# A hybrid SSD and attention layer: norm sums from token layout, paired SSD output weights, four-head v tiles and a third weight pair

## The chip, the core and the metric

The kernel is one launch on one core of a Trainium2 chip. The core has five engines with instruction streams of their own: TensorE (PE) for matmuls, VectorE (DVE), ScalarE (ACT), GpSimd (POOL) and SyncE (SP), which here issues most DMAs. They work on SBUF (128 partitions) and on PSUM, where matmuls put their sums. The metric is the time of one execution on the device in microseconds, as the median over runs; lower is better. The traces come from single profiled executions.

## What is computed

One decoder layer on 512 tokens of width 1024, in float32. The input is normalised and projected; the columns of the projection feed a Mamba-2 SSD mixer (16 heads, four chunks of 128 tokens) and a forgetting attention (16 heads of 64). Both results go through one output projection and are added to x; then come a second norm and a gated MLP with a causal convolution of width 3.

```python
h = rms_norm(x, norm_mix_w)
proj = h @ w_in
z, xbc, dt_raw, q, k, v, f_raw = jnp.split(
    proj, [Z_END, XBC_END, DT_END, Q_END, K_END, V_END], axis=-1)
y_ssd = ssd_mixer(xbc, z, dt_raw, ...)   # conv width 4, SiLU, chunked scan, gated group norm
y_fox = fox_mixer(q, k, v, f_raw, ...)   # q and k normed per head, decay added to the logits, softmax
mixed = jnp.concatenate([y_ssd, y_fox], axis=-1)
x = x + mixed @ w_out
hf = rms_norm(x, norm_ffn_w)
x = x + conv_gated_mlp(hf, w_up, ffn_conv_w, ffn_conv_b, w_down)
```

## The kernel before

**Precision.** Each large product is done in float32r, in three passes (`mm3`, lines 108 to 113): a value is split into a high part and the rest, and high x high, high x low and low x high are summed in PSUM. So every weight tile (128 x 1024) is loaded by SP into one of five `wraw` buffers, copied to its high part `wh` by ScalarE (line 104), and subtracted to its low part `wl` (line 105) by VectorE or POOL. `load_split` does this. Which engine subtracts is written out by hand in `LOW_PART` (line 36): each key is a kind of load, and the letters are taken in turn, `d` for VectorE and `p` for POOL; a key that is missing means POOL, and a call may name the engine itself. `wh` and `wl` have two buffers each.

**PSUM.** Eight banks of 128 x 512: three in the pool `g` (`bank()`: feature tiles, token blocks with two banks each, output projection), four in `m` (`mbank()`: scan, attention, transposes), one called `o`.

**The start.** x comes in transposed (`xT`, features on partitions), in eight blocks. Each is scaled by the norm's weight and split to `xh` and `xl` (line 180). The norm's factor per token comes later, since it is only a factor on the projection's results: it needs the sum of squares of each token. The squares of the eight blocks are taken by ScalarE (blocks 1, 3, 5, 7) and POOL (the others) at lines 203 to 208, added on VectorE (line 235), and summed over the partitions by four small matmuls with a column of ones into the bank `spin` (line 238). `token_scale` (line 137) turns the sums into `r`, the factor with tokens on partitions, and `R`, the same with tokens along the free axis: VectorE, a power on POOL, a diagonal on VectorE (line 140), a matmul with ones (line 144, `rbc`), a ScalarE copy (line 145).

**SSD.** `feature_tile` makes 128 columns of xbc for all tokens, in 24 matmuls. `early` (line 603) names tiles that are started ahead of `dt_f`, the chain for dt and the forget gates: tile 8 (made with the eight x blocks), 10 and 0. `ssd_proj` (line 336) makes the other tiles of a group of eight heads, multiplies each by R, runs the convolution and SiLU on VectorE and ScalarE and transposes; then it makes the gate z by token blocks. `ssd_scan` (line 386) runs over four chunks and leaves `m`, four feature blocks of 128 in high and low parts.

**Output projection.** `out_proj(pairs, m, halves)` (line 243) takes weight tiles of two feature blocks ("pair") by 512 columns ("half"). For each token block it sums over the pairs given to it in one bank and adds the bank to `x2`, which holds x in token layout (line 255). It was called with one pair at a time: pairs 0 and 1 for SSD group 0 while group 1 is scanned, pairs 2 and 3 for group 1, 4 to 7 for the attention groups.

**Attention.** `token_block` (line 319) makes q, k or v of four heads for all tokens in two banks, with 96 matmuls of 256 columns. `v_proj` (line 472) scales v by `r` and splits it, on ScalarE and VectorE in turn, for two heads at a time. Heads run in order; `fillers` (line 645) lists which projections are emitted ahead of which head.

**MLP.** 44 feature tiles up, gating, then a down projection of seven products; the weights' sums are built by accumulating DMAs of POOL's queue (line 730) whose descriptors use a scratch of 2048 bytes (line 973). `split_unit` (line 734) takes weight pairs from the two of `wp`, and each third from a pair in the pool `pb`.

**Order.** Each engine runs its instructions in a fixed order. It is made by the framework when the program is built: it simulates the kernel and takes what is ready, by priority; work under `high_priority` goes first, else what was emitted first. So an edit in one place can change the order elsewhere.

Of the kernel before, what the change touches and what calls it, by code (L numbers as in the profile page):

```python
# [8 lines left out]
F32 = mybir.dt.float32  # L9
# [46 lines left out]
def tile_hybrid_layer(  # L56
# [105 lines left out]
    first = [wp.tile([P, 1024], F32R, tag=t, name=t) for t in ("wh", "wl")]  # L162
# [34 lines left out]
    sqs = []  # L197
    for k in range(NK):
        xr = load_x(k)
        if k == 0:  # L200
            nc.sync.dma_start(pc[:, 0:NK], pcol[:, 0:NK])
        split_x(k, xr)
        sq = px.tile([P, SEQ], F32, tag="sq", name="sq", bufs=NK)
        if k in ACT_SQ:
            act.activation(sq, xr, AF.Square)
        else:
            pool.tensor_tensor(out=sq, in0=xr, in1=xr, op=ALU.mult)
        sqs.append(sq)
        if k in (1, 3):
            split_first(*load_first(k // 2))  # L210
# [22 lines left out]
    second = load_split(wxbc[10], sub=low_part("second"))  # L233
    for k in range(1, NK):
        dve.tensor_add(sqs[0], sqs[0], sqs[k])
    with tc.high_priority(AHEAD):
        for tb in range(NTB):
            pe.matmul(spin[:, tb : tb + 1], sqs[0][:, tb * P : (tb + 1) * P], ones[:, 0:1], start=True, stop=True)
        token_scale(r, R, spin[:, 0:NTB], px)
# [3 lines left out]
    def out_proj(pairs, m, halves=(0, 1)):  # L243
        for half in halves:
            ws = [load_split(wout[pair, half], sub=low_part("o%d" % pairs[0])) for pair in pairs]
            for tb in range(NTB):
                s = slice(tb * P, (tb + 1) * P)
                o = bank("po")
                for n, (h, l) in enumerate(ws):
                    for j in range(2):  # L250
                        k = 2 * n + j
                        c = slice(j * 512, (j + 1) * 512)
                        mm3(o, m[k][0][:, s], m[k][1][:, s], h[:, c], l[:, c], k == 0, k == 2 * len(pairs) - 1)
                dst = x2[:, tb, half * 512 : (half + 1) * 512]
                dve.tensor_add(dst, o, dst)  # L255
# [729 lines left out]
```

## Time and profile before

| what | value |
|---|---|
| median of 3 runs | 828.99 us (828.06 to 830.2) |
| the profiled execution | 829.39 us, its span 827.6 us |
| mean granted TensorE clock | 0.999 |
| DMA | 98.23 MB, mean 119 GB/s |
| weight splits, ScalarE part (line 104) | 103 of 1052 ns |

The span runs from the first to the last instruction. A group of instructions is shown as line, engine, operation, output<-inputs with partitions x elements, count, then busy time and mean duration in ns, then the idle time of the engine just before them and what ended it. PEld is TensorE's weight load, which overlaps its matmuls. A wait is shown as the engine and line that waited, what for, then us in total, times, longest. Matmuls are pipelined and their ends are modelled, so a busy TensorE is not one at its peak.

### The profile page before, as it was taken

The numbers are of one execution on the slowest core, as the hardware profiler recorded it, in microseconds if no ns is written. First come the engines' busy times: TensorE is split into PE (matmuls) and PEld (weight loads), VectorE is DVE, ScalarE is ACT, GpSimd is POOL, SyncE is SP. The second block draws the span as 40 slices with busy tenths as digits, with TensorE's granted clock in tenths as the row PEclk, the third lists the DMA queues.
The fourth block names the chain that finished last, engine by engine and source line by source line (L and its number), as shares of the span: only waits on it lengthen the run. The fifth ranks groups of instructions, "written<-read, shape, count | busy, mean of one in ns | idle before, by whom it ended". The sixth has DMA issues, their size and how long they took to land.

```text
span 827.6 us, 12438 instructions
## 1 busy us (share of the span) xinstructions
PE 807.4 (98%) x4599; PEld 698.7 (84%) x4599; DVE 629.7 (76%) x1017; ACT 437.2 (53%) x847; POOL 293.8 (36%) x281
## 2 busy tenths in 40 slices
PE   8999989899999999999999999999999999999997
PEld 5788879779999998798898888888888888888886
DVE  7597898676789788997988767667666666887844
ACT  5346655534478675684575364344443344556532
POOL 4125343364565445126132514322333333143120
PEclk9999999999999999999999999999999999999999
DMA  8424323241333332333322263332233223499983
GB/s 308 164 92 132 102 77 104 89 144 60 102 116 104 114 103 79 110 94 126 103 81 74 77 165 116 101 102 81 98 102 102 100 84 96 116 248 194 208 185 94
DMA packets 31405, 98.23 MB, mean 119 GB/s; under 512 B 4016, under 2 KB 5104, under 8 KB 31344
## 3 DMA queue, kind: packets, MB, share of 16 engines
q1 hardware_dynamic: 27456, 85.38, 31.8%
q0 software_dynamic: 3456, 11.54, 7.8%
q8 instruction: 36, 0.59, 0.3%
q10 hardware_dynamic: 432, 0.52, 0.2%
q14 instruction: 25, 0.20, 0.1%
HBM read 91.56 MB, written 2.20 MB: 113 GB/s over the span
## 4 chain that ended last, share of the span: by engine, by line
PE 80%; DVE 10%; issue 3%; ACT 3%; DMA 2%; POOL 1%; SPq 0%; DVEq 0%; POOLq 0%; ACTq 0%
PE up L111 29%; PE pq L111 16%; PE po L111 10%; PE Y L111 5%; PE Z L111 4%; PE X L111 4%; DVE xs L352 2%; PE g L111 2%; PE o L586 2%; PE pT L572 2%; DMA sc<-cs_d 1%; PE yd L416 1%; PE S L546 1%; PE S L545 1%; DVE wl L105 1%
## 5 line engine op out<-in xcount | busy, mean ns | idle before, releaser
L104 ACT CAST wh<-wraw 128x1024 fp32r<-128x1024 f32 x103 | 108.3, 1052 | 137.7 <-PE up L111 72.1
L111 PE MATMUL pq<-wh,xl 128*128 128x256 f32 x512 | 146.3, 286 | 0.0
L111 PE MATMUL pq<-wh,xh 128*128 128x256 f32 x512 | 146.0, 287 | 0.0
L111 PE MATMUL pq<-wl,xh 128*128 128x256 f32 x512 | 145.1, 284 | 0.0
L111 PE MATMUL up<-hh,wl 128*128 128x512 f32 (+1 forms) x368 | 140.2, 381 | 0.2 <-DVE wl L105 0.2
L111 PE MATMUL up<-hl,wh 128*128 128x512 f32 (+1 forms) x368 | 139.9, 380 | 0.0
L111 PE MATMUL up<-hh,wh 128*128 128x512 f32 (+1 forms) x368 | 139.8, 380 | 0.0
L105 POOL TENSOR_TENSOR wl<-wraw,wh 128x1024 fp32r<-128x1024 f32 x31 | 76.7, 2474 | 107.4 <-ACT wh L104 98.4
L105 DVE TENSOR_TENSOR wl<-wraw,wh 128x1024 fp32r<-128x1024 f32 x72 | 90.7, 1259 | 20.5 <-ACT wh L104 20.4
L111 PEld LDWEIGHTS pq<-wl,xh 128*128 128x128 f32 x512 | 97.6, 191 | 1.3 <-issue 0.5
L111 PEld LDWEIGHTS pq<-wh,xh 128*128 128x128 f32 x512 | 97.2, 191 | 1.8 <-issue 1.2
L111 PEld LDWEIGHTS pq<-wh,xl 128*128 128x128 f32 x512 | 97.6, 191 | 0.7 <-issue 0.5
L111 PEld LDWEIGHTS up<-hh,wl 128*128 128x128 f32 x368 | 69.2, 188 | 13.8 <-DVE wl L105 0.4
L111 PEld LDWEIGHTS up<-hh,wh 128*128 128x128 f32 x368 | 69.1, 188 | 13.2 <-issue 0.2
L111 PEld LDWEIGHTS up<-hl,wh 128*128 128x128 f32 x368 | 69.2, 188 | 13.0
L779 DVE TENSOR_TENSOR up<-up,R 128x512 f32<-128x512 f32 x44 | 30.3, 691 | 57.0 <-PE up L111 57.0
L784 DVE SCALAR_TENSOR_TENSOR ua<-up,pc,ua 128x511 f32<-128x511 f32 (+1 forms) x88 | 67.1, 765 | 3.2 <-ACT ua L782 1.7
L532 POOL TENSOR_SCALAR bias<-cum,tokS 128x256 f32<-128x256 f32 (+1 forms) x32 | 22.6, 715 | 84.4 <-DVE nm L547 84.4
L255 DVE TENSOR_TENSOR x<-po,x 128x512 f32<-128x512 f32 x64 | 43.2, 683 | 10.1 <-PE po L111 9.5
L740 ACT CAST wh<-T 128x1024 fp32r<-128x1024 f32 (+1 forms) x30 | 29.3, 977 | 37.5 <-PE Z L111 15.6
L741 DVE TENSOR_TENSOR wl<-T,wh 128x1024 fp32r<-128x1024 f32 (+1 forms) x30 | 33.7, 1132 | 19.7 <-ACT wh L740 19.7
L794 POOL TENSOR_TENSOR ua<-ua 128x512 f32<-128x512 f32 x11 | 15.0, 1365 | 93.7 <-DVE ua L784 93.7
(239 smaller groups left out, 1885.2 us busy)
## 6 DMA issues: line engine op xcount, KB each, us to landing
wraw<-in_wup_dram SPq DMA_DIRECT2D x44, 512.0 KB, 3.3
wraw<-in_wqkv_dram SPq DMA_DIRECT2D x24, 512.0 KB, 3.4
T<-in_wdown_dram POOLq DMA_DIRECT2D x20, 512.0 KB, 7.4
wraw<-in_wout_dram SPq DMA_DIRECT2D x16, 512.0 KB, 3.4
wraw<-in_wxbc_dram SPq DMA_DIRECT2D x11, 512.0 KB, 4.0
T<-in_wdown_dram SPq DMA_DIRECT2D x10, 512.0 KB, 5.0
wraw<-in_wdown_dram SPq DMA_DIRECT2D x10, 512.0 KB, 3.6
wraw<-in_wz_dram SPq DMA_DIRECT2D x8, 512.0 KB, 3.6
```

Of the source, the lines that this page charges most:

```text
L104: act.copy(h, r)
L105: (sub or dve).tensor_tensor(out=l, in0=r, in1=raw(h), op=ALU.subtract)
L111: ins = pe.matmul(o, a, b, start=start and n == 0, stop=stop and n == 2, **kw)
L255: dve.tensor_add(dst, o, dst)
L352: dve.scalar_tensor_tensor(out=dst[:, s:], in0=xp[:, : SEQ - s], scalar=half_w[:, cw + 3 - s : cw + 4 - s], in1=dst[:, s:], op0=ALU.mult, ...
L532: (dve if qb == 2 else pool).tensor_scalar(out=b, in0=cum[:, :n], scalar1=-1.0, scalar2=edge, op0=ALU.mult, op1=ALU.add)
L572: pe.transpose(t[:, w : w + P], prob[:, o : o + P], ident)
L586: pe.matmul(cols[:m], v[:, kb, lh, vc], pt[:, s], start=kb == 0 and n == 0, stop=kb == NTB - 1, skip_group_check=True,)
L740: act.copy(h[:, :n], src[:, :n])
L741: dve.tensor_tensor(out=l[:, :n], in0=src[:, :n], in1=raw(h[:, :n]), op=ALU.subtract)
L779: dve.tensor_mul(xp, o, R2)
L784: dve.scalar_tensor_tensor(out=a[:, s:], in0=xp[:, : SEQ - s], scalar=pc[:, cw + 2 - s : cw + 3 - s], in1=a[:, s:], op0=ALU.mult, op1=ALU.add,
```

## The change

The sums of squares come from x in token layout: x2 is loaded ahead of the feature tiles, and ScalarE squares each token block with a running sum (`accum_out`), in place of eight squares, seven additions and four small matmuls. A third weight pair is split early (weights 10 and 0, now both on VectorE), and feature tile 1 joins the tiles started ahead of `dt_f`, in a bank of the pool `m`. The output projection takes the two pairs of an SSD group together: two token blocks at a time, over both weight tiles, with one addition each. v is one tile for four heads. `wh` and `wl` have three buffers everywhere, and the pair in `pb` is gone. `LOW_PART` is adapted, the fillers `a` and `b` become the two column halves `a0` and `a1` of pairs 2 and 3, and the scratch of POOL's DMA queue is halved.

```diff
-ACT_SQ = (1, 3, 5, 7)
 LOW_PART = {
     "feat": "pddddddddp",
-    "o0": "dp",
-    "o2": "dp",
+    "o0": "d",
+    "o2": "d",
     "o4": "pd",
     "o5": "pd",
+    "o6": "pd",
     "o7": "pd",
...
-        h = wp.tile([P, 1024], F32R, tag="wh", name="wh")
-        l = wp.tile([P, 1024], F32R, tag="wl", name="wl")
+        h = wp.tile([P, 1024], F32R, tag="wh", name="wh", bufs=3)
+        l = wp.tile([P, 1024], F32R, tag="wl", name="wl", bufs=3)
...
-        sq = px.tile([P, SEQ], F32, tag="sq", name="sq", bufs=NK)
-        if k in ACT_SQ:
-            act.activation(sq, xr, AF.Square)
-        else:
-            pool.tensor_tensor(out=sq, in0=xr, in1=xr, op=ALU.mult)
-        sqs.append(sq)
...
-    second = load_split(wxbc[10], sub=low_part("second"))
-    for k in range(1, NK):
-        dve.tensor_add(sqs[0], sqs[0], sqs[k])
+    second, third = [load_split(wxbc[j], sub=dve) for j in (10, 0)]
+    for tb in range(NTB):
+        nc.sync.dma_start(x2[:, tb, :], x[tb * P : (tb + 1) * P, :])
     with tc.high_priority(AHEAD):
+        ssx = px.tile([P, NTB], F32, tag="ssx", name="ssx")
         for tb in range(NTB):
-            pe.matmul(spin[:, tb : tb + 1], sqs[0][:, tb * P : (tb + 1) * P], ones[:, 0:1], start=True, stop=True)
-        token_scale(r, R, spin[:, 0:NTB], px)
+            sq = px.tile([P, D], F32, tag="sq", name="sq", bufs=2)
+            act.activation(sq, x2[:, tb, :], AF.Square, accum_out=ssx[:, tb : tb + 1])
+        token_scale(r, R, ssx, px)
...
-            for tb in range(NTB):
-                s = slice(tb * P, (tb + 1) * P)
-                o = bank("po")
+            banks = {}
+            for t0 in (0, 2):
                 for n, (h, l) in enumerate(ws):
-                    for j in range(2):
-                        k = 2 * n + j
-                        c = slice(j * 512, (j + 1) * 512)
-                        mm3(o, m[k][0][:, s], m[k][1][:, s], h[:, c], l[:, c], k == 0, k == 2 * len(pairs) - 1)
-                dst = x2[:, tb, half * 512 : (half + 1) * 512]
-                dve.tensor_add(dst, o, dst)
+                    for tb in (t0, t0 + 1):
+                        s = slice(tb * P, (tb + 1) * P)
+                        if n == 0:
+                            banks[tb] = bank("po")
+                        for j in range(2):
+                            k = 2 * n + j
+                            c = slice(j * 512, (j + 1) * 512)
+                            mm3(
+                                banks[tb], m[k][0][:, s], m[k][1][:, s], h[:, c], l[:, c],
+                                k == 0, k == 2 * len(pairs) - 1,
+                            )
+                        if n == len(ws) - 1:
+                            dst = x2[:, tb, half * 512 : (half + 1) * 512]
+                            dve.tensor_add(dst, banks[tb], dst)
...
-        v = [pa.tile([P, NTB, 2, 2 * HD], F32R, tag="v", name="v", bufs=4) for _ in range(2)]
-        for pr in range(2):
-            for tb in range(NTB):
-                c = (tb % 2) * 256 + pr * P
-                o = tiles[tb // 2][:, c : c + P].rearrange("p (h d) -> p h d", d=HD)
-                act.activation(v[pr][:, tb, :, 0:HD], o, AF.Copy, scale=r[:, tb : tb + 1])
-                dve.scalar_tensor_tensor(
-                    out=v[pr][:, tb, :, HD:], in0=o, scalar=r[:, tb : tb + 1], in1=raw(v[pr][:, tb, :, 0:HD]),
-                    op0=ALU.mult, op1=ALU.subtract,
-                )
+        v = pa.tile([P, NTB, 4, 2 * HD], F32R, tag="v", name="v", bufs=2)
+        for tb in range(NTB):
+            c = (tb % 2) * 256
+            o = tiles[tb // 2][:, c : c + 256].rearrange("p (h d) -> p h d", d=HD)
+            act.activation(v[:, tb, :, 0:HD], o, AF.Copy, scale=r[:, tb : tb + 1])
+            dve.scalar_tensor_tensor(
+                out=v[:, tb, :, HD:], in0=o, scalar=r[:, tb : tb + 1], in1=raw(v[:, tb, :, 0:HD]),
+                op0=ALU.mult, op1=ALU.subtract,
+            )
...
-    early = {8: b0, 10: feature_tile(second), 0: feature_tile(wxbc[0], po.tile([P, 512], F32, tag="o", name="j0"))}
+    early = {8: b0, 10: feature_tile(second), 0: feature_tile(third, po.tile([P, 512], F32, tag="o", name="j0"))}
+    early[1] = feature_tile(wxbc[1], mbank("j1"))
...
-    for tb in range(NTB):
-        nc.sync.dma_start(x2[:, tb, :], x[tb * P : (tb + 1) * P, :])
     st1 = ssd_proj(1)
-    for pair in range(2):
-        out_proj((pair,), m0[2 * pair : 2 * pair + 2])
+    out_proj((0, 1), m0)
...
-    fillers = {0: ["q1"], 3: ["v1"], 4: ["q2", "v2"], 5: ["o0"], 8: ["q3"], 9: ["a", "o1"], 10: ["v3"], 12: ["o2"], 15: ["b"]}
+    fillers = {
+        0: ["q1"], 3: ["v1"], 4: ["q2", "v2"], 5: ["o0"], 8: ["q3"], 9: ["a0", "o1"], 10: ["v3"], 12: ["o2"],
+        15: ["a1"],
+    }
...
-        if name == "a":
-            out_proj((2,), m1[0:2])
-        elif name == "b":
-            out_proj((3,), m1[2:4])
+        if name[0] == "a":
+            out_proj((2, 3), m1, halves=(int(name[1:]),))
...
-        where = pb if turn[0] % 3 == 2 else wp
-        turn[0] += 1
-        h = where.tile([P, 1024], F32R, tag="wh", name="wh")
-        l = where.tile([P, 1024], F32R, tag="wl", name="wl")
+        h = wp.tile([P, 1024], F32R, tag="wh", name="wh", bufs=3)
+        l = wp.tile([P, 1024], F32R, tag="wl", name="wl", bufs=3)
...
-    nc = _bacc.Bacc("TRN2", target_bir_lowering=False, num_devices=1, dynamic_dma_scratch_size=2048)
+    nc = _bacc.Bacc("TRN2", target_bir_lowering=False, num_devices=1, dynamic_dma_scratch_size=1024)
```

More of the change, by code (lines that the diff above doesn't have):

```diff
@@ L161, in tile_hybrid_layer @@
     px = px_ctx.enter_context(tc.tile_pool(name="px", bufs=1))
-    first = [wp.tile([P, 1024], F32R, tag=t, name=t) for t in ("wh", "wl")]
+    first = [wp.tile([P, 1024], F32R, tag=t, name=t, bufs=3) for t in ("wh", "wl")]
     wdt = px.tile([P, NK, 64], F32R, tag="wdt", name="wdt")
@@ L196, in tile_hybrid_layer @@
     load_dt()
-    sqs = []
     for k in range(NK):
@@ L558, in fox_values @@
     def fox_values(head, prob, v, osum):
-        lh = head % 2
+        lh = head % 4
         own, other = HALVES[head % 2]
@@ L640, in end_head @@
         with urgent():
[L641 removed]
+            m = fox_values(n, probs.pop(n), vs[n // 4], pairs[n // 2][2])
         if m is not None:
             mf.append(m)
[L645 removed]
+    fillers = {
+        0: ["q1"], 3: ["v1"], 4: ["q2", "v2"], 5: ["o0"], 8: ["q3"], 9: ["a0", "o1"], 10: ["v3"], 12: ["o2"],
+        15: ["a1"],
+    }
     def fill(name):
[L648 to L651 removed]
+        if name[0] == "a":
+            out_proj((2, 3), m1, halves=(int(name[1:]),))
         elif name[0] == "q":
```

2 lines of the change are left out of this document (removed).

## The prediction

> **What bounds the kernel now.** I read the head of the page first: engine shares, then the chain of work that ended last.
>
> ```profile
> PE 807.4 (98%) x4599; PEld 698.7 (84%) x4599; DVE 629.7 (76%) x1017; ACT 437.2 (53%) x847; POOL 293.8 (36%) x281
> PE 80%; DVE 10%; issue 3%; ACT 3%; DMA 2%; POOL 1%; SPq 0%; DVEq 0%; POOLq 0%; ACTq 0%
> ```
>
> TensorE is busy 807.4 of 827.6 us and carries 80% of the chain. The change leaves the large matmuls as they are, so it can win only what TensorE idles, plus the few matmuls it removes. Where it idles is in the stretches of the run, cut where stages change (us of stretch, then busy time and instruction count of each engine, clock, DMA share, GB/s):
>
> ```profile
> 0.00:23.19 23.19, 18.72 (x65) 12.11 (x65) 16.13 (x23) 12.32 (x20) 9.78 (x13) 1.00 0.87 319
> 23.19:70.00 46.81, 44.57 (x259) 38.80 (x259) 38.40 (x68) 21.78 (x46) 10.23 (x5) 1.00 0.31 104
> 70.00:170.00 100.00, 94.65 (x594) 82.42 (x593) 81.04 (x109) 54.91 (x139) 41.52 (x30) 1.00 0.33 108
> 170.00:310.00 140.00, 140.00 (x1070) 132.84 (x1069) 109.77 (x225) 87.52 (x202) 77.54 (x78) 1.00 0.33 103
> 310.00:340.00 30.00, 26.77 (x196) 24.54 (x194) 25.98 (x52) 18.20 (x43) 11.62 (x15) 1.00 0.29 97
> 340.00:477.08 137.08, 136.84 (x862) 120.90 (x860) 119.79 (x252) 81.23 (x175) 47.75 (x52) 1.00 0.29 91
> 477.08:827.60 350.52, 345.82 (x1567) 287.06 (x1567) 238.56 (x293) 161.20 (x225) 95.37 (x91) 1.00 0.48 129
> ```
>
> Idle TensorE time (first number minus second) is 4.5 us in the start, 2.2 us up to 70, 5.4 us up to 170 (SSD scan of group 0), nothing up to 310, 3.2 us around 325 and 0.2 us after. The last stretch loses 4.7 us, and the next view, of what TensorE waited for, has next to nothing from there: that loss is the tail after the last matmul. So the MLP, 350 us, is closed to this change. What TensorE waited for:
>
> ```profile
> PE yT L447 <- DVE y L442: 1.7, 1, 1.7
> PE pt L307 <- DVE cs L305: 1.5, 1, 1.5
> PE po L111 <- ACT msh L449: 1.5, 1, 1.5
> PE g L213 <- DVE xl L183: 1.4, 1, 1.4
> PE qkT L497 <- DVE tok L469: 1.3, 1, 1.3
> PE po L111 <- DVE v L480: 1.2, 1, 1.2
> PE po L111 <- ACT th L376: 1.1, 1, 1.1
> ...
> PE xT L361 <- DVE xs L357: 0.8, 1, 0.8
> PE g L238 <- DVE sq L235: 0.8, 1, 0.8
> ...
> PE up L111 <- DVE wl L105: 0.2, 1, 0.2
> ```
>
> All rows shown but two end on VectorE. The only wait for a weight split (`wl`) in the whole view is the last, 0.2 us. A third weight pair alone is therefore worth about nothing.
>
> **The start.** One row a timeline instruction: start, duration, engine, line, tile, idle before.
>
> ```profile
> 14.48 3.52 DVE L183 SCALAR_TENSOR_TENSOR xl<-xr,pc,xh 128x512 fp32r<-128x512 f32 x2
> 14.78 2.67 POOL L105 TENSOR_TENSOR wl<-wraw,wh 128x1024 fp32r<-128x1024 f32 x1 [1.98 <-ACT wh L104]
> 22.27 1.05 PE L238 MATMUL g<-ones,sq 128*128 128x1 f32 x8 [0.76 <-DVE sq L235]
> 22.44 2.38 POOL L105 TENSOR_TENSOR wl<-wraw,wh 128x1024 fp32r<-128x1024 f32 x1 [4.99 <-ACT wh L104]
> 25.85 0.69 DVE L140 TENSOR_TENSOR diag<-ident,r 128x512 f32<-128x512 f32 x1 [2.33 <-POOL r L123]
> 30.82 1.02 PE L144 MATMUL rbc<-diag,ones 128*128 128x512 f32 x2
> 31.88 0.59 ACT L145 COPY R<-rbc 128x512 f32<-128x512 f32 x1 [1.58 <-PE rbc L144]
> ```
>
> Before, seven VectorE additions of squares stand among the eight `xl`, and the POOL subtraction for weight 10 stretches two `xl` to 3.52 us; TensorE loses 1.4 us there. Then it waits 0.8 us for the last addition and spends 22.27 to 23.19, 0.9 us, on the eight small sums; tile 10 starts only behind them, in the bank that they held. Gone are the additions, the small matmuls, and (weight 10 now on VectorE) the POOL block. **1.4 + 0.8 + 0.9 = 3.1 us off TensorE's path**, because tiles 10, 0 and now 1 follow at once. Next late would be the blocks of x: at the rates quoted under the next head (251 and 357 GB/s) they and weight 8, some 2.75 MB, are down by 11 us, five before the wait, so that does not take it back. Both ends: 0 (tile 8 slips to another cause) and 3.5. I take 3.1.
>
> **When R comes.** The first VectorE work on the feature tiles needs R, ready at 32.47 (31.88 + 0.59). Now R needs the token-layout x, whose four loads move ahead of the other weights on SP's queue; weights 1, 2 and 3 now stand behind 2 MB.
>
> ```profile
> 0.00:10.00 10.00, 7.83 (x24) 4.99 (x24) 3.94 (x7) 6.37 (x11) 3.56 (x10) 1.00 0.76 251
> 10.00:20.00 10.00, 8.47 (x28) 5.41 (x29) 10.00 (x12) 4.91 (x9) 5.48 (x3) 1.00 0.93 357
> L766 ACT ACTIVATE junk<-x 128x1024 f32<-128x1024 f32 x4 | 4.2, 1057 | 0.0
> ```
>
> By 20 us 2.5 + 3.6 = 6.1 MB had moved. Ahead of and including x stand, by shape: xT 2.1, weight 8 0.5, small tables 0.25, weights 10 and 0 1.05, x 2.1, sum 6.0 MB. So x lands at about 20 us. The squares are the same instruction as `junk`, 1.06 us each: done between 21.3 (they follow the loads) and 24.3 (all four wait). The scale then needs the small POOL power and `diag`: before, from 23.2 (the small sums done) to 26.5, while POOL was still on weight 0 until 24.8 (22.44 + 2.38), now on VectorE; without that wait an estimated 2.1 us. `diag` stands at 23.4 to 26.4 against 26.5. But the row of `rbc` shows more: it was ready at 26.5 and ran at 30.8, since TensorE's order is fixed when the program is planned. Placed when ready, R is there at 25 to 28, **about 6 us sooner**. ACT also carries more: four squares of 1.06 for four of 0.61, hidden, since ACT is busy 12.3 of the first 23.2 us. If the cover were gone, R would move by the 1.8 us.
>
> **What an earlier R is worth.** VectorE idles 8.4 of the 46.8 us of the second stretch, and until R it has little it may start. Six us of head start move its work forward, and TensorE has a fourth tile (24 matmuls, in a bank of the other pool) to cover: 5.6 us by the row of the chain below. The two waits of this stretch, `cs` 1.5 and `xs` 0.8, need less than 6 us. Ends: 0 and 2.2 (the idle time of the row). **I take 1.8.**
>
> **VectorE's load up to 170.** The costs of the moved operations:
>
> ```profile
> L105 POOL TENSOR_TENSOR wl<-wraw,wh 128x1024 fp32r<-128x1024 f32 x31 | 76.7, 2474 | 107.4 <-ACT wh L104 98.4
> L105 DVE TENSOR_TENSOR wl<-wraw,wh 128x1024 fp32r<-128x1024 f32 x72 | 90.7, 1259 | 20.5 <-ACT wh L104 20.4
> L255 DVE TENSOR_TENSOR x<-po,x 128x512 f32<-128x512 f32 x64 | 43.2, 683 | 10.1 <-PE po L111 9.5
> L461 ACT ACTIVATE tok<-pq,r 128x256 f32<-128x256 f32 x32 | 15.1, 472 | 8.0 <-PE pq L111 8.0
> L479 ACT ACTIVATE v<-pq,r 128x128 fp32r<-128x128 f32 x32 | 11.4, 365 | 15.8 <-DVE v L480 9.9 <-PE pq L111 5.6
> L480 DVE SCALAR_TENSOR_TENSOR v<-pq,r,v 128x128 fp32r<-128x128 f32 x32 | 10.9, 347 | 5.5 <-ACT v L479 5.2
> ```
>
> Over the whole run nine subtractions go from POOL to VectorE: seven in the output projection (pairs 0 to 3 leave one, two, one and two; pair 6 leaves one) and net two of the feature weights (10, 0 and 7 go to VectorE, 1 comes to POOL). VectorE gets 9 x 1.26 = 11.3 us. It loses 16 of the 64 output additions (four SSD pairs, 32 to 16) = 10.9, the seven square additions, 6.5 (counting stretched ones about 0.92 each), and in v 32 x 0.35 for 16 of about 0.42, 4.4. That is 10 us less VectorE work, and 9 x 2.47 + 5 = 27 us less POOL work. POOL matters through a second path:
>
> ```profile
> 182.85 4.20 PE po L111 x18
> 121.08 2.38 POOL L105 TENSOR_TENSOR wl<-wraw,wh 128x1024 fp32r<-128x1024 f32 x1
> 121.14 2.86 DVE L442 SCALAR_TENSOR_TENSOR y<-y,ss,nwb 128x512 f32<-128x512 f32 x1 [0.80 <-POOL ss L123]
> ```
>
> (The first row, of the chain, is for the pace of `po`: 0.233 us a matmul.) The VectorE instruction starts with POOL's and ends 0.5 us after it, and TensorE's longest wait (1.7, `yT`) is for it. So a POOL subtraction can cost VectorE up to its own length, 2.4 us, more than the 1.26 of doing it itself.
> [...]
> In this stretch weight 7 and three output weights leave POOL, weight 1 and the z weights stay there, so the very block at 121 (a z weight) may recur. The waits total 1.7 + 1.5 + 1.1 + 0.9 of smaller ones, 5.4 us by the stretch. Two of them (`msh`, `th`) are the output projection waiting for the end of scan 0; its fused form needs the last chunk 7 us in instead of 4.2 (30 against 18 matmuls). The head start of 6 us helps all. Ends: -2 (a new order brings new waits of the size of one here) and 5.4. **I take 2.5.**
>
> **Attention.** v now holds four heads: per group 4 pairs of operations of about 0.47 and 0.42 us for 8 of 0.37 and 0.35, taking turns, 8 x 0.72 less 4 x 0.89, some 2 us sooner out of the bank. It meets `po <- v` (1.2); `tok` (1.3) stays. Ends -1 and 3.2; **I take 1.0.** The fused output projection here is the same 48 matmuls per call, halves by column.
>
> **What costs.** Fused, the output projection holds two of three banks in place of one, and its second tile starts 6 matmuls (1.4 us) after the first. A token block before it holds two, emptied by ACT at 4 x 0.47 = 1.9 us a tile. 0.5 us at a boundary where ACT is on time; about half of six boundaries have SSD or attention work of TensorE between. Ends 0 and the rival's 14; **I take 1.0.** Three weight pairs in the MLP and the smaller scratch of POOL's DMA queue: no wait of TensorE after 478 touches either, so 0; ends -0.3 and +1.5 (one late accumulating load, as long as the longest wait here).
>
> **Sum.** 3.1 + 1.8 + 2.5 + 1.0 - 1.0 = 7.4 us. The profiled execution took 829.4 us (its span 827.6 and 1.8 around it), the median of the runs is 829.0. 829.4 - 7.4 = 822.0; 0.4 less for the median: **821.6 us**.
>
> **Rivals.**
> - *R no sooner.* `rbc` again sits behind a whole feature tile in TensorE's order, or x lands later. For it: it did so before by 4.3 us, and the added tile gives the plan more to put first. Against: VectorE idles then, and the scale has priority. Only the start and v remain, less the boundaries: 829.0 - 3.1 = **825.9**.
> - *Two of three banks.* Slower: at each of six boundaries between token blocks and the fused projection (into and out of three calls) TensorE waits for both tiles to be emptied, 3.8 us less the cover of 1.4: 6 x 2.4 = 14.4, less the gain without the 1.0, 8.4: +6, **835**. It decides from 1.4 us a boundary (8.4 / 6). For it: no bank wait could show before, with one bank held. Against: ACT is 59% to 63% busy in those stretches and the scan's or heads' matmuls, from the other pool, fill in.
> - *All waits go.* The head start carries through: idle time from 23 to 477, 2.2 + 5.4 + 3.2 + 0.2 = 11, with the start 14: **815**.
>
> **How the numbers follow.** Forecast (818 to 825) 0.55, R no sooner (825 to 828) 0.2, banks 0.13, all waits gone 0.12. About 0.3%, 2.5 us, is what a measurement of this kernel can tell from no change. Faster by that (under 826.5): 0.55 + 0.12 + 0.6 of the 0.2 = 0.79; same: the other 0.08 with 0.03 from mild bank waits, 0.11; slower 0.10. The range leaves out the bank rival and a little below: 814.5 to 829.
>
> **What would show it.** The start: no gap over 1 us before tile 10, which begins at about 20 us. R: its copy ends before 28. The scan: idle TensorE from 23 to 170 down from 7.6 to about 3.3 us. v: no wait of `po` for v. Banks: waits of `po` or `pq` for an ACT `tok` or a VectorE addition would speak for the rival. Wrong would be the whole sum if the new order of TensorE has waits of some us in the stretch from 170 to 310, which has none now.

## The result, and the profile after

The changed kernel takes 818.5 us (median of 4 runs, 818.03 to 818.96) beside 828.83 of the kernel before (4 runs). The ratio is 0.9874, 95% interval 0.9856 to 0.9891, so 9.0 to 11.9 us are won, and the medians differ by 10.3; 7.4 were forecast. The profiled execution took 818.96 us, its span 817.2 against 827.6. First the page of the changed kernel, engine shares and the chain by engine, then its windows in the cuts of the prediction (the last one shown ends well before the MLP).

```profile
PE 803.1 (98%) x4591; PEld 697.9 (85%) x4591; DVE 610.4 (75%) x987; ACT 437.2 (54%) x835; POOL 265.9 (33%) x268
PE 85%; DVE 10%; DMA 2%; ACT 1%; issue 1%; POOL 0%; SPq 0%; DVEq 0%; ACTq 0%
```

```profile
0.00:23.19 23.19, 21.12 (x74) 15.10 (x75) 10.84 (x20) 16.50 (x25) 2.77 (x9) 1.00 0.89 326
23.19:70.00 46.81, 42.46 (x256) 37.29 (x255) 40.88 (x66) 22.37 (x46) 12.17 (x5) 1.00 0.34 111
70.00:170.00 100.00, 97.55 (x601) 84.88 (x601) 79.26 (x113) 55.99 (x141) 35.42 (x27) 1.00 0.32 109
170.00:310.00 140.00, 140.00 (x1090) 133.85 (x1089) 107.50 (x221) 89.38 (x204) 74.52 (x82) 1.00 0.34 106
310.00:340.00 30.00, 30.00 (x203) 27.21 (x202) 25.97 (x58) 18.93 (x42) 11.78 (x14) 1.00 0.35 105
```

Subtract the second number from the first, as before. TensorE idles 2.1 us in the start (4.5 before), **4.4 up to 70 (2.2)**, 2.5 up to 170 (5.4), nothing up to 310, and nothing around 325 (3.2). So the stretch that an earlier R was to help got worse, and the others better. From 23 to 170 us the idle time is 6.8 us (7.6 before), where the prediction named 3.3 as its sign. What TensorE waited for in the changed kernel:

```profile
PE xT L363 <- ACT b_tok L370: 1.5, 1, 1.5
PE xT L363 <- ACT x_tok L368: 1.4, 1, 1.4
PE xT L363 <- DVE xs L359: 1.4, 1, 1.4
PE xT L363 <- ACT wh L104: 1.3, 1, 1.3
PE g L195 <- DVE mhalf L131: 1.0, 1, 1.0
...
PE po L111 <- DVE x L257: 0.3, 1, 0.3
```

The waits of before for `y`, `xl`, `cs`, `msh`, `tok`, `v` and `th` are gone. Three new ones, 4.3 us, stand before transposes (`xT`) of feature tiles, at 52, 58 and 64 us. The last is for a tile that VectorE has not finished; the first two are for ScalarE, which empties the one bank that all these transposes use and was itself waiting for VectorE just before (3.5 and 2.7 us). The fourth row, `wh`, falls in the scan (119 us). Only 0.3 us is a wait for a bank of the output projection, at 456 us, in the call of an attention pair.

The same milestones in both profiled executions show where the time was won (in both, the trace records TensorE's full clock from 13.8 or 13.9 us on, so they can be compared from the start; the first matmul listed is of tile 0 before and of tile 10 after):

| milestone | before | after | won so far |
|---|---|---|---|
| first matmul behind tile 8 and the sums | 23.19 | 19.26 | 3.9 |
| first `yd` (scan of group 0) | 85.5 | 83.2 | 2.3 |
| last `yT` of that scan | 160.0 | 155.6 | 4.4 |
| first `up` (MLP) | 473.7 | 464.7 | 9.0 |
| first `Y` (down projection) | 716.8 | 707.4 | 9.4 |
| end of the span | 827.6 | 817.2 | 10.4 |

Of the 10.4 us, 6.1 are idle time of TensorE (20.2 us to 14.1) and 4.3 busy time. The busy part holds the small matmuls (four in the code, eight instructions in the profile, 0.9 us), the output projection and the down projection. Counted from each matmul's start to the next one's, without idle time, the same 384 matmuls of the output projection take 91.9 us in place of 93.8. In the down projection the products come faster; the chain has them one by one, first before and then after:

```profile
716.98 15.08 PE Y L111 x66
```

```profile
707.60 14.96 PE Y L111 x66
```

At 0.12 to 0.16 us for each of its seven products that is about 1 us. The timeline of the changed kernel shows when R came (start, duration):

```profile
19.26 0.40 PE L111 MATMUL g<-xh,wh 128*128 128x512 f32 x1
22.41 0.69 DVE L140 TENSOR_TENSOR diag<-ident,r 128x512 f32<-128x512 f32 x1 [0.46 <-POOL r L123]
30.16 1.02 PE L144 MATMUL rbc<-diag,ones 128*128 128x512 f32 x2
31.22 0.59 ACT L145 COPY R<-rbc 128x512 f32<-128x512 f32 x1
```

`diag` was ready at 23.1, a little ahead of the forecast (23.4 to 26.4), and `rbc` still ran at 30.2, seven microseconds later, because TensorE's fixed order has it there, behind the whole of tiles 10 and 0 (TensorE isn't idle in between). R came at 31.8 instead of 32.47: 0.7 us sooner, not 6.

### The profile page after: what moved, and what is told of

Its sections match the earlier page's. It is cut to its first block, busy times and chain, and to the rows that moved or that the text cites. A ratio compares the mean times of both kernels' runs of the same rounds, so it can differ in the third digit from the quotient of the medians.

```text
span 817.2 us, 12396 instructions
## 1 busy us (share of the span) xinstructions
PE 803.1 (98%) x4591; PEld 697.9 (85%) x4591; DVE 610.4 (75%) x987; ACT 437.2 (54%) x835; POOL 265.9 (33%) x268
## 4 chain that ended last, share of the span: by engine, by line
PE 85%; DVE 10%; DMA 2%; ACT 1%; issue 1%; POOL 0%; SPq 0%; DVEq 0%; ACTq 0%
PE up L111 29%; PE pq L111 19%; PE po L111 10%; PE Y L111 6%; PE X L111 4%; PE Z L111 4%; DVE xs L354 3%; PE o L587 2%; PE pT L573 2%; PE g L111 2%; PE S L547 1%; PE S L546 1%; DVE wl L105 1%; PE yd L418 1%; DVE xp L347 1%; DVE cT L354 1%
## 5 line engine op out<-in xcount | busy, mean ns | idle before, releaser
L111 PE MATMUL pq<-wh,xl 128*128 128x256 f32 x512 | 148.3, 290 | 0.0
L105 DVE TENSOR_TENSOR wl<-wraw,wh 128x1024 fp32r<-128x1024 f32 x81 | 104.0, 1284 | 32.3 <-ACT wh L104 27.9
L111 PEld LDWEIGHTS up<-hl,wh 128*128 128x128 f32 x368 | 69.2, 188 | 13.4 <-issue 0.2
L105 POOL TENSOR_TENSOR wl<-wraw,wh 128x1024 fp32r<-128x1024 f32 x22 | 54.0, 2459 | 71.8 <-ACT wh L104 57.2
L552 ACT ACTIVATE prob<-prob,nm 128x128 f32<-128x128 f32 (+1 forms) x64 | 35.9, 564 | 24.9 <-DVE nm L548 24.8
```

The lines of the kernel that those rows point to most:

```text
L105: (sub or dve).tensor_tensor(out=l, in0=r, in1=raw(h), op=ALU.subtract)
L111: ins = pe.matmul(o, a, b, start=start and n == 0, stop=stop and n == 2, **kw)
L552: act.activation(p, p, AF.Exp, scale=-1.0, bias=nm[:, qb : qb + 1], accum_out=sm[:, qb : qb + 1])
```

## The experiments

My theory at this point: the gain is the start, and fewer waits that come from a changed order of work rather than from the edit that was meant to remove each. The rivals: the fused projection, the v tile or the third pair earn their part themselves; or an earlier R is worth what was forecast, if it only came. Ratios are against the kernel before on the same chip (the changed kernel: 0.9874; run again, 0.9870).

### The parts undone one by one

**Norm sums as before** (squares of blocks, seven additions, eight small matmuls; all else as changed):

```diff
+        sq = px.tile([P, SEQ], F32, tag="sq", name="sq", bufs=NK)
+        if k in ACT_SQ:
+            act.activation(sq, xr, AF.Square)
+        else:
+            pool.tensor_tensor(out=sq, in0=xr, in1=xr, op=ALU.mult)
+        sqs.append(sq)
...
-        token_scale(r, R, ssx, px)
+        token_scale(r, R, spin[:, 0:NTB], px)
```

> The changed kernel with the norm sums as before: squares of the eight transposed blocks on ScalarE and POOL, seven additions on VectorE, small matmuls into the bank spin, x in token layout loaded late. All else as changed (weight 10 and 0 on VectorE, three pairs, tile 1 early). If the start pays where its waits stood, tile 10 begins some 2 us later than the 19.2 us of the changed kernel (the wait for the last addition and the small matmuls return, 1.7 us; the POOL block on the two xl does not, since weight 10 stays on VectorE), and the time is 820.2 to 821.5. Rival: the gain at the start is weight 10's subtraction leaving POOL, then the time stays within 1 us of 818.5. Rival: all of it is the norm sums, then tile 10 begins near 23.2 and the time is 822.5 or more.

822.7 us, ratio 0.9912 (0.9897 to 0.9927). The start is worth 0.0038 to 0.0042 of 829, **3.1 to 3.5 us**. Its first `yd` stands at 86.2 and its first `up` at 468.0, 3.0 and 3.3 us later than in the changed kernel, and its three waits of `xT` are the same; so the loss arises at the start and is carried to the end unchanged. Two things limit this reading. In this profile the clock was at half from 9.0 to 15.8 us (0.83 granted over 0 to 20 us; matmuls 0.43 us apart, 0.23 behind it), 2 us longer into the run than in the changed kernel's (13.9), which is worth an estimated 1 us, half of that time. And R is 3.0 us later too (34.8), so the run prices the norm sums whole, not the small matmuls apart from R.

**One pair at a time in the output projection**, with the fillers and low parts of before:

```diff
-    out_proj((0, 1), m0)
+    for pair in range(2):
+        out_proj((pair,), m0[2 * pair : 2 * pair + 2])
...
-    "o0": "d",
-    "o2": "d",
+    "o0": "dp",
+    "o2": "dp",
```

> The changed kernel with the output projection as before: one weight pair at a time, one addition per pair, fillers a and b, the entries of LOW_PART for it as before (four of its SSD subtractions on DVE fewer, six more on POOL, pair 6 all on POOL). If the fused projection pays through the waits that are gone (the two of po at the end of scan 0, 2.6 us, and the three around 325 us, 3.2 us), the time is 821 to 825 and these waits return. Rival, that two of three banks cost as much as the additions save: 817.5 to 819.5. Rival, that the waits at 325 us went with v for four heads: about 821, and only the waits of po at the end of scan 0 return.

817.32 us, 0.9848 (0.9832 to 0.9864). The fused projection earns nothing that shows; the waits of `po` that the kernel before had (`msh`, `th`) didn't come back.

**v for two heads at a time**, as before:

```diff
-        v = pa.tile([P, NTB, 4, 2 * HD], F32R, tag="v", name="v", bufs=2)
+        v = [pa.tile([P, NTB, 2, 2 * HD], F32R, tag="v", name="v", bufs=4) for _ in range(2)]
```

> The changed kernel with v made for two heads at a time, as before: eight pairs of ScalarE and VectorE operations a group for four. If the four-head v removed the waits around 325 us, the wait of po for v returns (1.2 us) and with it part of the others: 819.5 to 822. Rival, that the fused projection or the shift of the whole order removed them: within 0.7 us of 818.5.

817.61 us, 0.9858 (0.9837 to 0.988): nothing, and no wait of `po` for v. That wait was a matter of the order.

**Nine more low parts on POOL, as before** (weights 10, 0 and 7 and seven of the output projection's go back, weight 1 goes to VectorE):

```diff
-    second, third = [load_split(wxbc[j], sub=dve) for j in (10, 0)]
+    second, third = [load_split(wxbc[j], sub=pool) for j in (10, 0)]
...
-    "feat": "pddddddddp",
-    "o0": "d",
+    "feat": "ddddddddp",
+    "o0": "dppp",
```

> The changed kernel with the weight subtractions back on the engines they had before: weights 10 and 0 on POOL and 1 on VectorE, of the eight of the fused output projection six on POOL, pair 6 on POOL (nine more on POOL in all). If POOL's subtraction costs VectorE more than doing it itself, the two xl are stretched again ahead of tile 8's end, tile 10 begins 1 us or more later for the same clock, and the time is 820 to 823. Rival, by durations alone (nine times 1.26 us less on VectorE): 817 to 818.5. Rival, the engine doesn't matter behind TensorE: 818 to 819.

818.86 us, 0.9884 (0.987 to 0.9899): 0 to 1 us, and the intervals overlap, so no worth is shown. The stretched `xl` that the prediction put at 1.4 us didn't come back with weight 10 on POOL: without the squares VectorE is done with all eight `xl` at 13.2 us, and POOL's subtraction starts at 14.3.

### R made to come sooner

**`rbc` fixed behind 18 of tile 10's 24 matmuls.** Feature tile 10 is emitted in two parts with the norm between them, and kept in that order:

```diff
+    t10 = feature_tile(second, ks=range(6))
     with tc.high_priority(AHEAD):
...
         token_scale(r, R, ssx, px)
+    feature_tile(second, t10, range(6, NK), pin=True)
```

> The changed kernel with the matmul that spreads the norm's factor (rbc) pinned in TensorE's order behind 18 of the 24 matmuls of tile 10, where its input has been ready, in place of behind the whole of tiles 10 and 0 (30.2 us); tile 0 is pinned behind the rest of tile 10. R is then there at about 24.5 us in place of 31.8. If an R that is 7 us sooner gives VectorE a head start that TensorE can use, the three waits for xT between 50 and 65 us (4.3 us in the changed kernel) shrink to at most 1.5 and the time is 814 to 816.5. Rival, that VectorE and ScalarE catch up whatever R does, or that weights are late: 817.5 to 819.5. Rival, that the pin brings a wait of TensorE of its own, since the factor is later than it: over 819.5, with a wait of rbc for diag.

822.14 us, 0.991 (0.9884 to 0.9935): slower than the changed kernel by 3 us in the middle, though the intervals just touch. The timeline of this kernel, in order (its profiled execution, 824.9 us, was the slowest of four):

```profile
23.09 2.33 POOL L105 TENSOR_TENSOR wl<-wraw,wh 128x1024 fp32r<-128x1024 f32 x1
23.14 2.84 DVE L140 TENSOR_TENSOR diag<-ident,r 128x512 f32<-128x512 f32 x1 [0.95 <-POOL r L123]
26.03 2.07 PE L144 MATMUL rbc<-diag,ones 128*128 128x512 f32 x2 [3.03 <-DVE diag L140]
```

POOL's low part of weight 1 started 0.05 us ahead of `diag`, which took 2.84 us in place of 0.69, and TensorE now had to wait for it.

**The same without that neighbour**: `rbc` behind tile 10 and two of eight steps of tile 0, weight 1 split on VectorE.

```diff
+    t10 = feature_tile(second)
+    t0 = feature_tile(third, po.tile([P, 512], F32, tag="o", name="j0"), range(2), pin=True)
...
+    feature_tile(third, t0, range(2, NK), pin=True)
```

> As the run with the early rbc, but the matmul stands six matmuls later (behind tile 10 and two of the eight steps of tile 0), and weight 1 is subtracted on VectorE, so that POOL doesn't hold up diag. If that run lost its time to the 3.0 us wait for diag and to the slow clock behind it, both are gone here, R is there by 25.5 us, and the time is 814 to 817.5. Rival, that an early R doesn't pay because the order made for it has TensorE wait for cs (3.1 us there): 818.5 to 821 and that wait stays.

This does what the forecast wanted, R at 24.6:

```profile
22.80 1.13 PE L144 MATMUL rbc<-diag,ones 128*128 128x512 f32 x2 [0.55 <-DVE diag L140]
24.04 0.58 ACT L145 COPY R<-rbc 128x512 f32<-128x512 f32 x1
```

The changed kernel's repeat, below, is as far in the start (74 matmuls in its first 20 us for 77 here, 60 in the first execution) and is the fair comparison: R is 4.0 us sooner than there (24.6 for 28.6), the first `yd` 5.5 (74.5 for 80.0). And the time is 820.75 us, 0.9912 (0.9896 to 0.9927), **some 3 us worse**, which the split of weight 1 on VectorE doesn't explain (the next experiment has it too). Its waits:

```profile
PE xT L366 <- DVE xs L362: 3.1, 3, 1.5
PE yT L452 <- DVE y L447: 2.4, 2, 2.2
PE xT L366 <- ACT x_tok L371: 1.4, 1, 1.4
```

The lead is lost step by step: 5.5 us at the first `yd`, 2.0 at the last `yT` of that scan, and at the first `up` this kernel is 3.4 us behind the repeat. Over the whole run TensorE idles 1.5 us more than there (16.6 to 15.1) and is busy 1.9 us longer; 1.0 of that is the slow pace behind the wait for `y` (five matmuls 0.43 us apart in place of 0.23; last section). So R came sooner, and the order of TensorE made for it has other waits. Both runs with a pinned `rbc` change that order too, so they don't price an earlier R by itself; a run further down has one without a pin.

**The stretched VectorE steps at 40 to 65 us.** In the changed kernel each of the three waits of `xT` follows a VectorE step of 2.0 to 2.9 us beside a split on POOL (at 45.7, 52.9 and 58.5 us), the third one these:

```profile
58.54 2.73 POOL L105 TENSOR_TENSOR wl<-wraw,wh 128x1024 fp32r<-128x1024 f32 x1 [3.27 <-ACT wh L104]
58.92 2.89 DVE L354 SCALAR_TENSOR_TENSOR xs<-xp,half_w,xs 128x509 f32<-128x509 f32 x1
```

The same operation takes 0.74 us elsewhere in that stretch. So the splits of weight 1 and of the first z block went to VectorE:

```diff
-    "feat": "pddddddddp",
+    "feat": "dddddddddd",
+    "z0": "dddd",
```

> The changed kernel with five more subtractions on VectorE: feature weight 1 and the four weights of z of group 0. In the run with the early rbc, VectorE's diag stood 2.84 us in place of 0.69 beside POOL's subtraction of weight 1, and two convolution steps 2.9 us in place of 0.75 beside those of z. If that blocking is what delays VectorE between 32 and 70 us, the stretched steps go, the waits for xT and cs between 50 and 70 us (5.5 us lost in the changed kernel) fall by half, and the time is 815 to 817.5. Rival, by durations: VectorE is full there, five times 1.26 us come on top and the time is 820 or more.

The local effect is whole, as one window shows, first of the changed kernel, then of this one, where TensorE idles nothing:

```profile
20.00:70.00 50.00, 45.65 (x270) 39.93 (x269) 41.99 (x69) 24.56 (x50) 13.58 (x6) 1.00 0.38 125
```

```profile
20.00:70.00 50.00, 50.00 (x322) 45.31 (x321) 41.34 (x78) 29.08 (x61) 3.09 (x3) 1.00 0.43 149
```

And yet the time is 816.91 us, 0.9869 (0.9853 to 0.9886), the same as the changed kernel. Most of the gain is given back in the scan, where waits come to 4.2 us (2.4 in the changed kernel), these two first, with 1.2 us of slow pace behind the second (six matmuls some 0.42 us apart in place of 0.23):

```profile
PE xT L364 <- ACT x_tok L369: 2.0, 1, 2.0
PE yT L450 <- DVE y L445: 1.6, 1, 1.6
```

**This together with the single-pair projection** (the two diffs joined) asked whether two neutral edits add up.

> The changed kernel with the output projection one pair at a time (as before) and with feature weight 1 and the weights of z of group 0 subtracted on VectorE: the two edits that each came out at or below the changed kernel. If they act in different places (the waits for xT and cs up to 70 us, and the order from 170 us on), they add: 814.5 to 816.5. Rival, that what VectorE wins up to 70 us is given back in the scan up to 240 us, whatever the projection: 816.5 to 819.

818.78 us, 0.9882 (0.9865 to 0.99): they don't. The profiled execution has a single long wait in the scan, the first of its list (it took 821.88 us, the slowest of five, so how much of that wait the others had isn't shown):

```profile
PE yT L442 <- DVE y L437: 4.9, 1, 4.9
```

### The third weight pair

**Two pairs in the changed kernel**, the third one of the MLP in the pool `pb` again:

```diff
-        h = wp.tile([P, 1024], F32R, tag="wh", name="wh", bufs=3)
-        l = wp.tile([P, 1024], F32R, tag="wl", name="wl", bufs=3)
+        h = wp.tile([P, 1024], F32R, tag="wh", name="wh")
+        l = wp.tile([P, 1024], F32R, tag="wl", name="wl")
```

> The changed kernel with two weight pairs, as before (in the down projection each third from the other pool again); weight 0 is split when tile 8's pair is free. If the third pair is worth next to nothing by itself, TensorE doesn't wait for wl, and the time is within 1 us of 818.5, but for the stretch after the attention, which took 353.9 us before and 352.5 in the changed kernel: if the place of the third pair in the down projection is the cause, it goes back to 353.9 and the time is 819.5 to 820.5. Rival, that the third pair is what feeds the fused output projection and tile 0: 821 to 824, with waits of po or j for wl.

826.18 us, 0.9978 (0.9965 to 0.999): **7.7 us lost**, most of the whole gain. Its waits are for weights, and one row for 20 to 460 us counts the idle time, of this kernel and then of the changed one:

```profile
PE pq L111 <- POOL wl L105: 4.5, 2, 3.2
PE xT L363 <- DVE xs L359: 2.4, 2, 1.5
PE po L111 <- DVE wl L105: 1.4, 1, 1.4
```

```profile
20.00:460.00 440.00, 427.17 (x2876) 386.95 (x2875) 356.38 (x666) 256.22 (x581) 160.22 (x164) 1.00 0.33 103
```

```profile
20.00:460.00 440.00, 432.73 (x2912) 391.73 (x2911) 355.72 (x670) 258.64 (x583) 165.42 (x166) 1.00 0.33 105
```

12.8 us idle, against 7.3; another 1.5 us goes in the slow pace behind the longest wait (last section) and 1 us or so in the down projection. Does the third pair then earn 7.7 us?

**The third pair alone in the kernel before** (its POOL queue's scratch halved too, which makes the room):

```diff
-        h = wp.tile([P, 1024], F32R, tag="wh", name="wh")
+        h = wp.tile([P, 1024], F32R, tag="wh", name="wh", bufs=3)
...
-dynamic_dma_scratch_size=2048)
+dynamic_dma_scratch_size=1024)
```

> The kernel before with the third weight pair alone: three buffers for wh and wl everywhere, the extra pair of the down projection gone, POOL's scratch 1024 bytes (which makes the room). Norm sums, output projection, v and tile 1 as before. If the third pair is worth what its removal from the changed kernel cost (7 to 8 us), the time is 821 to 823.5. If it is worth something only where the other parts lean on it, since the kernel before did not wait for wl (0.2 us in all), only the down projection gains its 1.1 us: 826.5 to 828.5.

830.25 us (12 runs), 1.0015 (1.0001 to 1.0029): no gain. Weight 0 is now split early as well, on POOL, right behind weight 10, and the timeline of this kernel shows what stood beside it:

```profile
14.47 3.53 DVE L183 SCALAR_TENSOR_TENSOR xl<-xr,pc,xh 128x512 fp32r<-128x512 f32 x2
14.83 5.39 POOL L105 TENSOR_TENSOR wl<-wraw,wh 128x1024 fp32r<-128x1024 f32 x2 [2.04 <-ACT wh L104]
17.92 2.85 DVE L235 TENSOR_TENSOR sq<-sq 128x512 f32<-128x512 f32 x1
```

The wait of TensorE for `xl` (1.4 us before) and the window around 325 us, where before idled 3.2:

```profile
PE g L213 <- DVE xl L183: 4.4, 6, 1.4
```

```profile
310.00:345.00 35.00, 34.34 (x251) 32.07 (x250) 30.66 (x67) 22.38 (x52) 16.64 (x16) 1.00 0.33 106
```

So no gain here is a sum. Beside the kernel before, the first `yd` comes 0.6 us later, the last `yT` of that scan 2.4, the first matmul of the attention's logits 4.6; then the stretch around 325 us and the down projection win, and the end is 1.2 us later. What the third pair would be worth with these two early splits on VectorE, as the changed kernel has them, was not run.

**Two pairs and the single-pair projection** in the changed kernel (the diffs of both joined):

> The changed kernel with two weight pairs and with the output projection one pair at a time as before. If it is the fused projection that needs the third pair, its waits for wl (2.3 us of po with two pairs) go and the time is 818.5 to 821.5. If the order with the norm sums and tile 1 needs it, the 4.5 us wait of the token blocks for POOL's wl stays and the time is 823 to 827.

818.02 us, 0.9874 (0.9859 to 0.9889): all of the gain is there. The same row for 20 to 460 us:

```profile
20.00:460.00 440.00, 434.04 (x2919) 394.21 (x2918) 365.00 (x682) 259.09 (x583) 184.43 (x175) 1.00 0.33 105
```

6.0 us idle. So the third pair and the fused projection together are worth nothing measurable. The timelines show why the fused form needs the third pair. It holds two weight pairs through a call, and of the 6.8 us between the two runs 4.5 are waits for splits in or right behind such a call: at 169 us, between its two halves, at 185 and 187, for the next token block, and at 458, for the next pair. The single form has none of them. Of the rest 1.5 us stand ahead of the first call; the wait at 72 us, 3.2 us long, is not the projection's, since it is there with the single form too (2.3).

This run shows one thing more, about R:

```profile
24.61 0.59 ACT L144 COPY R<-rbc 128x512 f32<-128x512 f32 x1 [0.40 <-PE rbc L143]
```

With two pairs tile 0's weight is split later, and the planned order has `rbc` near the start of that tile: R is there at 25.2 us without any pin. (The fused form with two pairs has it at 23.9.) Beside the kernel with the single form and three pairs, whose R is at 30.5, the lead is 5.2 us at the first `yd` (76.7 for 81.9), and 1.8 at the first `up` (462.3 for 464.1), with no gain in the time (0.9874 and 0.9848). So an earlier R need not cost anything, and most of its lead doesn't reach the MLP. The two kernels differ in the third pair as well, so this isn't a clean price of R.

### The changed kernel once more

> The changed kernel itself, beside the other three on one chip, as the measure for them: 817.5 to 819.5, 0.986 to 0.989 of the kernel before. By the theory that the start depends on when the clock of TensorE is granted in full (between 7 and 16 us in the runs so far), its executions spread over 2 us and more; by the rival, that the spread is the chip's, they lie within 1 us on one chip.

817.91 us (816.54 to 819.54), 0.9870 (0.9854 to 0.9885). One program, one chip, 3 us of spread; R comes at 28.6 in this profile, since all of TensorE's order runs 3.2 us earlier. The last section shows one source of the spread.

## Why the prediction was right, and where it was not

The sign held, the time lies within the range, and the gain was 10.3 us where 7.4 were forecast. That the size comes so near is in part luck: one term had the wrong sign, others came out by a path that the prediction didn't name, and some 3 us of the gain are busy time that it didn't count.

- **Start, 3.1.** Right in size: 3.9 in the two profiles, 3.1 to 3.5 by undoing the norm sums. The blocks of x didn't become late; tile 10 began at 19.3 (20 forecast). The split of the sum was not right: 1.4 of it were put down to POOL's subtraction of weight 10, but the norm sums alone carry the whole.
- **R about 6 us sooner, worth 1.8.** Wrong in both halves; this is the step that failed. The price of the scale was right (`diag` at 23.1), but what places `rbc` is TensorE's planned order, not the moment at which it is ready: R came 0.7 us sooner. That is the rival "R no sooner", by its own mechanism. Its 825.9 us didn't follow, since the scan and the stretch around 325 us won 6.1 us of idle time without an earlier R. The stretch that the 1.8 us were to come from lost 2.2 instead. And an R that is really sooner isn't worth 1.8: at 24.6, pinned, the kernel is some 3 us slower; at 25.2, with two pairs and no pin, the time is that of the changed kernel. The step took VectorE's free time and the idle time of two waits for something that a head start fills.
- **Scan, 2.5.** The idle time from 70 to 170 us fell by 2.9, a little more than forecast; not by the head start, which wasn't there.
- **Attention, 1.0.** The 3.2 us around 325 did go whole, the upper end of the term, but not through v: with v as before they stay away, and the third pair alone takes these three waits away as well.
- **Banks, a cost of 1.0.** One wait of 0.3 us for an output addition, none of `pq` or `po` for `tok`. The rival of 835 us has no trace.
- **Third pair, about nothing alone.** Net, so it came out (with the early splits on POOL), but not because nothing changed. What the step left out is that the fused projection needs the third pair: taken from the changed kernel it costs 7.7 us, of which 4.5 us are waits in or right behind the fused calls. I had charged the fused form with banks; its price is the weight buffers that it holds.
- **MLP, 0.** Some 1 us was won. The first product of 66 matmuls takes 15.08 us in the three kernels with the pair in `pb` (before, two pairs, two pairs with the single projection) and 14.96 in the eleven where all three pairs lie in `wp`; why isn't shown. That no wait stands in a stretch doesn't close it.
- **VectorE's load.** Forecast 10 us less, measured 19.3. By groups, the edits give +13.4 (splits) - 10.7 (additions) - 6.5 (squares) - 3.4 (v) = -7.2. The other 12 are in operations that the change leaves as they are: the mean `xl` takes 750 ns for 1104, the scaling of `tok` 1782 for 2139. That POOL stretched fewer of them, with 265.9 us of work for 293.8, fits the rows above, but wasn't shown one by one.

What stays open: norm sums are 3.1 to 3.5 us, the down projection about 1, projection, third pair and v nothing. Some 5 to 6 us remain. The profiles show where they are won (2.9 us of idle time in the scan of group 0, 3.2 around 325 us, 1.9 of busy time in the output projection, less 2.2 lost up to 70 us), not by which edit. The kernel with two pairs and the single projection has the same time. It shares with the changed one the norm sums, feature tile 1 ahead of `dt_f`, weights 10 and 0 on VectorE (0 to 1 by undoing) and the v tile, but not the whole order: its R is sooner, and it waits elsewhere. So it doesn't prove that the rest lies in what they share. Tile 1 alone was not undone on the chip, so its part isn't shown. No version tried is shown to beat the changed kernel: the best two ratios, 0.9848 and 0.9858, have intervals that overlap with its own.

## What to carry to other kernels

On an engine that is 98% busy in a fixed order, price an edit by undoing it in the finished kernel and by doing it alone: the third pair was worth nothing alone, 7.7 us in the company of the fused projection, and nothing together with it. A result that is ready earlier is used earlier only if the bounding engine's order has a place for it, and a scan started 5.5 us sooner can still leave a later end (both shown here for one kernel). What is saved in one stretch may come back as one wait in the next, so compare milestones to the end, not only the stretch.

## What the runs showed of the hardware

**Half clock behind some waits.** In the kernel with two pairs, after its longest wait, rows of the timeline (the operation is the same; the spacing goes from 0.12 to 0.21 us), then the window of the slow ones, with a granted clock of 0.50:

```profile
72.48 0.38 PE L111 MATMUL pq<-wl,xh 128*128 128x256 f32 x1 [3.19 <-POOL wl L105]
...
73.66 0.28 PE L111 MATMUL pq<-wl,xh 128*128 128x256 f32 x1
73.78 0.28 PE L111 MATMUL pq<-wh,xl 128*128 128x256 f32 x1
...
74.23 0.42 PE L111 MATMUL pq<-wh,xl 128*128 128x256 f32 x1
74.45 0.41 PE L111 MATMUL pq<-wh,xh 128*128 128x256 f32 x1
```

```profile
74.00:77.30 3.30, 3.30 (x18) 3.30 (x17) 2.08 (x2) 3.30 (x10) 0.00 (x0) 0.50 0.34 129
```

The slow spacing stands from 74.0 to 77.4: 16 matmuls at 0.21 us in place of 0.12, so a wait of 3.2 us cost an estimated 1.5 more. In the kernel with two pairs and the single projection it stands from 72.1 to 75.3, behind a wait of 2.34, and in the first of the two kernels with an early `rbc` from 61.8 to 66.7, behind one of 3.09. Over all the kernels from 32 to 180 us, no wait of up to 1.54 us had this behind it; of eleven from 1.63 to 4.91 us eight had, all five above 2.1 among them. In the start it followed shorter ones: with the third pair alone, two waits in sequence (0.52 and 1.44 us; spacing 0.23 us between them, 0.43 from 18.0 on), and then one of 0.98 behind eight small matmuls (0.43 us from 28.5 on). A long window hides it: 70 to 130 us of the kernel with two pairs has a granted clock of 0.97. What decides which waits have it behind them isn't shown.

**The clock at the start differs between executions.** In the first profiled execution of the changed kernel the trace records the full clock from 13.9 us on, and three rows show the spacing fall from 0.41 to 0.23 us; in the repeat it is 0.24 us at 7.7 us already:

```profile
13.54 0.56 PE L111 MATMUL g<-xh,wh 128*128 128x512 f32 x1
13.95 0.40 PE L206 MATMUL g<-xl,wdt 128*32 128x512 f32 x1
14.18 0.40 PE L111 MATMUL g<-xl,wh 128*128 128x512 f32 x1
```

```profile
7.73 0.40 PE L111 MATMUL g<-xl,wh 128*128 128x512 f32 x1
7.97 0.39 PE L206 MATMUL g<-xl,wdt 128*32 128x512 f32 x1
```

Every milestone up to the first `yd` is 3.2 us sooner in the repeat, and its span is 2.4 us shorter. Other kernels differ in this too: before, the spacing is 0.43 us up to 13.4 us and 0.23 from 13.8 on, and with the norm sums as before 0.43 from 10.4 to 15.6 and 0.23 from 15.9 on; over 0 to 20 us the granted clock is 0.83 with those sums and 0.91 in the runs with the single projection alone and with nine low parts on POOL. What decides this isn't shown. With 3.2 us between two executions of one program it is as large as most of the parts tested here, and the reason why medians, not profiles, price them.

**A small VectorE operation beside POOL.** Besides `diag` (0.69 us, 2.84 beside POOL), the scaling of four numbers a partition was stretched too. In the changed kernel it stands beside a subtraction on POOL from 22.8 to 25.4 us:

```profile
23.02 2.36 DVE L235 TENSOR_SCALAR rhalf<-r 128x4 f32<-128x4 f32 x1
```

It takes 0.16 us in the first kernel with an early `rbc`, behind the end of POOL's split. Both stretched operations end with POOL's or a little behind it: the scaling at 25.4 us with POOL at 25.4, `diag` at 26.0 with POOL at 25.4.
